# Softmax probabilities and attention heads turned through DRAM in a hybrid decoder layer

## The chip, the cores and the metric

The kernel runs on one core of one Trainium2 chip. The metric is the device time of one execution in microseconds (us); the time before is 1804.2 us, the median of three runs (1803.72 to 1804.21). Besides those runs there is one profiled execution, from which all durations below are read.

Engine names in the rows: PE is TensorE (matrix products and transposes by a product with the identity), DVE is VectorE, ACT is ScalarE, POOL is GpSimd, SP is SyncE, which here only issues DMAs. Each engine works through its own list of instructions strictly in order.

## The reference

One decoder layer on x (256 tokens, width 2048) and a memory of 256 tokens:

```python
x = x + 0.5 * swiglu(rms_norm(x, ffn1_norm), ffn1_gate, ffn1_up, ffn1_down)    # FFN a, inner width 5632

h = rms_norm(x, mix_norm)
fq, fk, fv, f_logit, sq, sk, sv, mq = split(h @ w_in)        # 768,768,768,6,768,256,256,512 columns
fq, fk = rms_norm per head (128 wide)                        # group A: 6 heads
out_a  = causal softmax(fq fk^T * scale + c[t] - c[s]) fv    # c = cumsum(log_sigmoid(f_logit + bias))
sq, sk = rms_norm per head                                   # group B: 6 query heads, 2 key/value heads
out_b  = softmax over a window of 128 (+ ALiBi, + a sink logit in the denominator) sv
mk, mv = rms_norm(mem) @ w_mem_k, rms_norm(mem) @ w_mem_v    # group C: 4 heads into the memory
mq, mk = rms_norm per head
out_c  = softmax(mq mk^T * scale) mv
x = x + concat(out_a, out_b, out_c) @ w_out
x = x + 0.5 * swiglu(rms_norm(x, ffn2_norm), ffn2_gate, ffn2_up, ffn2_down)    # FFN b
```

All in float32. Both attention products need their operands with the contracted index on the partitions: the heads of q and k as (128 of the head, tokens), and the probabilities as (keys, queries). They come out of the products before them the other way round, so they have to be transposed: this is what the change is about.

## The kernel before

**Weights.** Every projection streams its weight from HBM in groups of two 128-row tiles (`load_w`, L212): SP issues one DMA into `raw` (4 buffers, L218), ACT rounds it to `hi` (3 buffers, L220), DVE computes `lo = raw - hi` (3 buffers, L221). TensorE makes float32 accuracy of three faster products: for each of two 128-token tiles and each weight tile x_hi·hi (L315), x_hi·lo (L316) and x_lo·hi (L317), 12 matmuls in a group. So TensorE can't begin a group before ACT has cast it, nor pass the first product before DVE has its `lo`; and ACT can cast a group only once TensorE has left the group three before it, whose `hi` buffer it takes.

**Stages.** FFN a; then the mix stage (about 728 to 985 us): projections mk, mv (of the memory), mq, sqa, skv, sqb, fqa, fka, fqb, fkb, fva, fvb, eight groups each, 512 columns wide for the first three and skv, about 384 for the others; then w_out (wo); then FFN b.

**Attention beside the projections.** Small work is written as generators: `lanes.run` starts a free one, `lanes.put` queues an item for one of two lanes with the names it needs. After each weight group `lanes.tick()` steps every one of them, and a `yield n` skips n ticks. From this program order a scheduler of the framework makes the order on each engine when the kernel is compiled; at run time nothing can be overtaken on an engine.

**Heads.** When a projection is complete in PSUM, `heads_T` (L540) takes for every head and token tile a square with a row sum on ACT (L549, `junkh`; six in a 384-wide projection), a 14-step rsqrt on DVE (L201 to L210 and L554), a scaled copy to `q` on ACT (L559), the transposes on TensorE back into PSUM (L565), and a copy with the gain out of PSUM into `qkv` or `mkT` (L567).

**Probabilities.** A softmax item (`logits`, L676; `mem_stages`, L757) holds one lane from its logits (s_w, s_f, s_m) through maximum (L692), exponentials (L707, L774), normalising (L631), TensorE transposes of the probabilities (L717, L783: pt_w, pt_f, pt_m) and a copy from PSUM. For the sliding window (w0, w2, w4) and the memory (m0, m2) the same item goes on to the values (o_w, o_m) and to `mixT`.

**Turning through DRAM.** The kernel before already uses another transpose for FFN activations and for x: `turn_out` (L256) does 32x32 block transposes on DVE (L262) and writes four DMAs to DRAM (`far`, L268); one DMA reads them back (`turn_in`, L274) so that a strided read (`turned`, L278) gives the transpose. All five DMAs go on SP's queue, the one that also loads all weights.

Of the kernel before, what the change touches and what calls it, by code (L numbers as in the profile page):

```python
# [8 lines left out]
F32 = mybir.dt.float32  # L9
# [69 lines left out]

@with_exitstack  # L80
def hybrid_layer(ctx, tc, x, mem, ffn1_norm, ffn1_gate, ffn1_up, ffn1_down, mix_norm, mem_norm,
# [33 lines left out]
    graw1 = cpool.tile([NK, P], F32, name="graw1")  # L115
# [37 lines left out]
    tri = tri3[:, 0:P]  # L153
# [102 lines left out]
    def turn_out(tmp, src, name):  # L256

        for t in range(NT):  # L260
# [275 lines left out]
    with tc.tile_pool(name="mix", bufs=1, reuse_waits="tile") as mx, \  # L536
# [3 lines left out]
        def heads_T(acc, nh, r, gi, dst, name, off=0):  # L540

            q = mt.tile([P, 4 * SEQ], F32, tag="q", name=f"q_{name}").rearrange("p (t w) -> p t w", t=NT)
            s = small.tile([P, NT, 4], F32, tag="hs", name=f"hs_{name}")
            cols = lambda h: slice(off + h * HD, off + (h + 1) * HD)
            nc.vector.memset(s, 1.0)
# [10 lines left out]
            yield 2  # L556
            for t in range(NT):
# [4 lines left out]
            tv = acc.rearrange("p a b -> p (a b)")[:, :nh * SEQ].rearrange("p (h s) -> p h s", h=nh)  # L562
            for h in range(nh):
                for t in range(NT):
# [8 lines left out]
        def turn_tile(n):  # L573
            return mt.tile([P, 4 * SEQ], F32, tag="q" if n.startswith("out") else "s", name=f"turn_{n}")

        def turns_x1():
            raws = [turn_tile(f"in_x1{c}") for c in range(2)]
            for c in range(2):
                nc.sync.dma_start(*turn_in(raws[c], fars[c]))
            far3 = yield from turn_out(turn_tile("out_x13"), xchunk(3), "x13")  # L580
            for c in range(2):
                yield from scaled(x1T, raws[c], 4 * c, G_MIX)
                raws.append(turn_tile(f"in_x1{c + 2}"))
                nc.sync.dma_start(*turn_in(raws[c + 2], (fars + [far3])[c + 2]))
            for c in (2, 3):
                yield from scaled(x1T, raws[c], 4 * c, G_MIX)
# [38 lines left out]
        def normalise(p, sm, segs, name):  # L625
# [3 lines left out]
            for i in range(2):  # L629
                for t in range(NT):  # L630
                    nc.vector.tensor_scalar(out=p[:, i, segs[t]], in0=p[:, i, segs[t]],  # L631
                                            scalar1=ri[:, t, i:i + 1], scalar2=None, op0=ALU.mult)
# [33 lines left out]
        def logits(tag, h0, qT, kT, fox, name):  # L666
# [8 lines left out]
            else:  # L675
                s = mt.tile([P, 4 * SEQ], F32, tag="s", name=f"ss_{name}")  # L676
                s = s.rearrange("p (i s) -> p i s", i=2)[:, :, 0:3 * P]
# [20 lines left out]
            yield 3  # L698
            if not fox:
                es = small.tile([P, NT, 2], F32, tag="es", name=f"es_{name}")  # L700
                nc.vector.tensor_tensor(out=es, in0=nm,
                                        in1=sink6[:, None, h0:h0 + 2].to_broadcast([P, NT, 2]),
                                        op=ALU.add)
                nc.scalar.activation(es, es, AF.Exp)
            for i in range(2):
                for t in range(NT):
                    nc.scalar.activation(s[:, i, SEG[t]], s[:, i, SEG[t]], AF.Exp,  # L707
                                         bias=nm[:, t, i:i + 1], accum_out=sm[:, t, i:i + 1])
            yield 3
            if not fox:  # L710
                nc.vector.tensor_tensor(out=sm, in0=sm, in1=es, op=ALU.add)
            normalise(s, sm, SEG, name)
            yield 1
# [5 lines left out]
            pTs[name] = s  # L719
            nc.scalar.copy(s, pp[:, :, 0:3 * P])  # L720
            yield 1

        pTs = {}

        def values(tag, h0, v, mix0, name):
# [17 lines left out]
        def swa_pair(h0):  # L743
# [4 lines left out]
            def stages(tag):  # L748
                yield from logits(tag, h0, lambda h: sqT[:, h, :], lambda h: skT[:, h // 3, :], False,
                                  f"w{h0}")  # L750
                yield from values(tag, h0, v, 6, f"w{h0}")
            return stages

        def mem_pair(h0):
            return lambda tag: mem_stages(tag, h0)

        def mem_stages(tag, h0):  # L757
# [6 lines left out]
            nm = small.tile([P, 2, NT], F32, tag="nmm", name=f"nm_{name}")  # L764
            yield 2
            nc.vector.tensor_reduce(out=nm, in_=sp.rearrange("p i (t s) -> p i t s", t=NT), axis=AX.X,
                                    op=ALU.max, negate=True)
            s = mt.tile([P, 4 * SEQ], F32, tag="s", name=f"ss_{name}").rearrange("p (i s) -> p i s", i=2)
            sm = small.tile([P, NT, 2], F32, tag="sm", name=f"sm_{name}")
            segs = [slice(t * SEQ, (t + 1) * SEQ) for t in range(NT)]  # L770
            yield 1
            for i in range(2):
                for t in range(NT):
                    nc.scalar.activation(s[:, i, segs[t]], sp[:, i, segs[t]], AF.Exp,  # L774
                                         bias=nm[:, i, t:t + 1], accum_out=sm[:, t, i:i + 1])
            yield 1
            normalise(s, sm, segs, name)
            yield 3
            pp = psum(tag, f"pt_{name}")
            for i in range(2):  # L780
                for t in range(NT):
# [124 lines left out]
```

## Time and profile before

| what | value |
|---|---|
| median of three runs | 1804.2 us |
| the profiled execution's own time | 1803.99 us |
| its span, first to last instruction | 1802.3 us |
| TensorE busy | 1792.4 us, 99% |
| VectorE busy | 976.4 us, 54% |
| ScalarE busy | 845.7 us, 47% |
| granted TensorE clock, mean | 1.00 |

The profiled execution is 0.2 us from the median; 1.7 us of its time lie outside the span. In a timeline row the first number is the start in us from the span's start, the second the time in us until the end (of all, where a row merges several), and brackets give the idle time of that engine before the row and what ended it. Neighbouring rows overlap, since engines are pipelined: the pitch from start to start is what work costs in a series. The granted clock 1.00 is the upper of TensorE's two levels, 2.4 GHz.

### The profile page before, as it was taken

What the parts mean: (1) busy time and instruction counts of PE and PEld (TensorE: products, weight loads), DVE (VectorE), ACT (ScalarE), POOL (GpSimd) and SP (SyncE); (2) the same over time, 40 slices, a digit from 0 to 9 for tenths busy, and PEclk for the clock granted to TensorE, in tenths of its full rate; (3) what the DMA queues carried; (4) which work ended last, traced back from release to release, by engine and by line L of the source; (5) the groups of instructions that cost most, each with busy time, mean ns of one, the idle gap of its engine ahead of it and who ended that gap; (6) DMA issues with size and microseconds to landing.
All of it is one profiled execution on the core that took longest, in us unless ns stands there. A gap on an engine that the chain in (4) does not pass through costs nothing.

```text
span 1802.3 us, 21677 instructions
## 1 busy us (share of the span) xinstructions
PE 1792.4 (99%) x8170; PEld 1507.2 (84%) x8170; DVE 976.4 (54%) x1197; ACT 845.7 (47%) x1149; POOL 12.1 (1%) x31
## 2 busy tenths in 40 slices
PE   9999999999999999999999999999999999999998
PEld 7888888888888888888999888888888888888887
DVE  5555555555555564645665565555555555544443
ACT  6444444444445443656666454444444444433332
POOL 2000000000000000000000000000000000000000
PEclk9999999999999999999999999999999999999999
DMA  7777777777787777765656586777777777666663
GB/s 240 217 219 214 220 214 218 217 216 218 227 252 234 231 220 239 223 176 152 183 151 185 176 257 188 217 216 222 222 225 223 217 219 214 218 200 198 206 205 128
DMA packets 228025, 379.16 MB, mean 210 GB/s; under 512 B 13834, under 2 KB 65360, under 8 KB 227792
## 3 DMA queue, kind: packets, MB, share of 16 engines
q1 hardware_dynamic: 226512, 375.36, 68.8%
q8 instruction: 64, 1.05, 0.2%
q0 software_dynamic: 528, 1.22, 0.2%
q10 hardware_dynamic: 880, 1.19, 0.2%
q14 instruction: 41, 0.34, 0.1%
HBM read 358.31 MB, written 19.41 MB: 210 GB/s over the span
## 4 chain that ended last, share of the span: by engine, by line
PE 98%; DVE 1%; ACT 1%; DMA 0%; issue 0%; POOL 0%; DVEq 0%; POOLq 0%; ACTq 0%
PE ua L316 4%; PE ua L317 4%; PE gb L317 4%; PE ub L317 4%; PE gb L315 4%; PE ub L315 4%; PE gb L316 4%; PE ub L316 4%; PE ua L315 4%; PE da L316 4%; PE db L316 4%; PE db L315 4%; PE da L317 4%; PE db L317 4%; PE da L315 4%; PE ga L316 4%
## 5 line engine op out<-in xcount | busy, mean ns | idle before, releaser
L221 DVE TENSOR_TENSOR lo_bd<-raw_bd,hi_bd 128x1024 fp32r<-128x1024 f32 x88 | 107.7, 1224 | 122.6 <-ACT hi_bd L220 122.5
L221 DVE TENSOR_TENSOR lo_bu<-raw_bu,hi_bu 128x1024 fp32r<-128x1024 f32 x88 | 107.8, 1225 | 119.5 <-ACT hi_bu L220 119.5
L221 DVE TENSOR_TENSOR lo_au<-raw_au,hi_au 128x1024 fp32r<-128x1024 f32 x88 | 107.8, 1225 | 114.2 <-ACT hi_au L220 114.2
L221 DVE TENSOR_TENSOR lo_ad<-raw_ad,hi_ad 128x1024 fp32r<-128x1024 f32 x88 | 107.5, 1223 | 104.7 <-ACT hi_ad L220 104.6
L220 ACT CAST hi_bd<-raw_bd 128x1024 fp32r<-128x1024 f32 x88 | 92.8, 1055 | 145.5 <-PE db L317 140.5
L221 DVE TENSOR_TENSOR lo_bg<-raw_bg,hi_bg 128x1024 fp32r<-128x1024 f32 x88 | 107.4, 1220 | 96.4 <-ACT hi_bg L220 95.6
L220 ACT CAST hi_bg<-raw_bg 128x1024 fp32r<-128x1024 f32 x88 | 92.8, 1055 | 142.1 <-PE gb L317 86.5
L221 DVE TENSOR_TENSOR lo_ag<-raw_ag,hi_ag 128x1024 fp32r<-128x1024 f32 x86 | 104.9, 1220 | 93.8 <-ACT hi_ag L220 92.9
L220 ACT CAST hi_ad<-raw_ad 128x1024 fp32r<-128x1024 f32 x88 | 92.8, 1054 | 131.7 <-PE da L317 121.5
L220 ACT CAST hi_ag<-raw_ag 128x1024 fp32r<-128x1024 f32 x86 | 90.7, 1055 | 135.9 <-PE ga L317 83.2
L220 ACT CAST hi_bu<-raw_bu 128x1024 fp32r<-128x1024 f32 x88 | 92.8, 1054 | 105.2 <-PE ub L317 78.9
L220 ACT CAST hi_au<-raw_au 128x1024 fp32r<-128x1024 f32 x88 | 92.5, 1054 | 102.6 <-PE ua L317 79.1
L316 PE MATMUL da<-lo_ad,hT_a 128*128 128x512 f32 x352 | 137.0, 389 | 0.8 <-DVE lo_ad L221 0.8
L316 PE MATMUL ua<-lo_au,x0T 128*128 128x512 f32 x352 | 137.0, 389 | 0.3 <-DVE lo_au L221 0.3
L316 PE MATMUL gb<-lo_bg,x2T 128*128 128x512 f32 x352 | 137.0, 389 | 0.0
L315 PE MATMUL gb<-hi_bg,x2T 128*128 128x512 f32 x352 | 136.9, 389 | 0.0
L317 PE MATMUL ua<-hi_au,x0T 128*128 128x512 f32 x352 | 136.9, 389 | 0.0
L315 PE MATMUL da<-hi_ad,hT_a 128*128 128x512 f32 x352 | 136.9, 389 | 0.0
L317 PE MATMUL da<-hi_ad,hT_a 128*128 128x512 f32 x352 | 136.9, 389 | 0.0
L317 PE MATMUL gb<-hi_bg,x2T 128*128 128x512 f32 x352 | 136.9, 389 | 0.0
L315 PE MATMUL ub<-hi_bu,x2T 128*128 128x512 f32 x352 | 136.9, 389 | 0.0
L316 PE MATMUL ub<-lo_bu,x2T 128*128 128x512 f32 x352 | 136.9, 389 | 0.0
(478 smaller groups left out, 3934.9 us busy)
## 6 DMA issues: line engine op xcount, KB each, us to landing
raw_au<-in_ffn_up_dram SPq DMA_DIRECT2D x88, 512.0 KB, 4.5
raw_ad<-in_ffn_down_dram SPq DMA_DIRECT2D x88, 512.0 KB, 5.0
raw_bg<-in_ffn_gate_dram SPq DMA_DIRECT2D x88, 512.0 KB, 4.5
raw_bu<-in_ffn_up_dram SPq DMA_DIRECT2D x88, 512.0 KB, 4.4
raw_bd<-in_ffn_down_dram SPq DMA_DIRECT2D x88, 512.0 KB, 4.6
raw_ag<-in_ffn_gate_dram SPq DMA_DIRECT2D x86, 512.0 KB, 4.5
raw_wo<-in_w_out_dram SPq DMA_DIRECT2D x16, 512.0 KB, 5.2
far_a<-turn_out_a SPq DMA_DIRECT2D x44, 128.0 KB, 2.6
```

The costliest lines, as they stand in the source:

```text
L220: nc.scalar.copy(h, r)
L221: nc.vector.tensor_tensor(out=l, in0=r, in1=h.bitcast(F32), op=ALU.subtract)
L315: nc.tensor.matmul(acc[:, t, :w], hi, wh, start=first, stop=False)
L316: nc.tensor.matmul(acc[:, t, :w], hi, wl, start=False, stop=False)
L317: nc.tensor.matmul(acc[:, t, :w], lo, wh, start=False, stop=last)
```

## The change

The same numbers are computed. Eight of the nine head transposes (all but fkb) and the probabilities of m0, m2, w0, w2, w4 and f0 (not f2, f4) leave TensorE: they are turned by DVE and DMAs through DRAM, as the FFN activations are. Logits and values become separate lane items, so a softmax's lane is free while the turn is under way. A class `Slots` hands out the buffers (one `q`, two `s`, two `turn`) in the order in which they were asked for. The third chunk of x1T is turned in place in a `turn` tile. To make room, `junk`, `junkh` and the first gain load share one buffer, `ones` becomes a slice of `tri3`.

```diff
+class Slots:
+    def __init__(self, n):
+        self.n, self.asked, self.taken, self.back = n, 0, 0, set()
+    def take(self):
+        i, self.asked = self.asked, self.asked + 1
+        while self.taken < i or i >= self.n and i - self.n not in self.back:
+            yield 1
+        self.taken += 1
+        return i
+    def give(self, i):
+        self.back.add(i)
...
-            junk = small.tile([P, 512], F32, tag="junk", bufs=2, name="junk")
+            junk = small.tile([P, 512], F32, tag="junk", bufs=1, name="junk")
...
+        slots = {"q": Slots(1), "s": Slots(2), "turn": Slots(2)}
+        def take(tag, name):
+            i = yield from slots[tag].take()
+            return i, mt.tile([P, 4 * SEQ], F32, tag=tag, bufs=slots[tag].n, name=name)
+        def turn(src, name, out):
+            i, tmp = yield from take("turn", f"turn_{name}")
+            far = yield from turn_out(tmp, src, name, 1)
+            nc.sync.dma_start(*turn_in(tmp, far))
+            yield 3
+            yield from out(tmp)
+            slots["turn"].give(i)
...
-                    junk = small.tile([P, HD], F32, tag="junkh", bufs=2, name="junkh")
+                    junk = small.tile([P, 512], F32, tag="junk", bufs=1, name="junkh")[:, 0:HD]
...
-            tv = acc.rearrange("p a b -> p (a b)")[:, :nh * SEQ].rearrange("p (h s) -> p h s", h=nh)
-            for h in range(nh):
-                for t in range(NT):
-                    nc.tensor.transpose(tv[:, h, t * P:(t + 1) * P], q[:, t, h * HD:(h + 1) * HD], ident)
-            yield 1
-            nc.scalar.activation(dst, tv, AF.Copy, scale=gT[:, G_HEAD + gi:G_HEAD + gi + 1])
+            def out(tmp):
+                nc.scalar.activation(dst.rearrange("p h (c s) -> p h c s", s=32), turned(tmp, NT, nh), AF.Copy,
+                                     scale=gain)
+                yield 1
+            i, tmp = yield from take("turn", f"turn_{name}")
+            stages = turn_out(tmp, q, name, 1)
+            yield next(stages)
+            slots["q"].give(iq)
+            far = yield from stages
+            nc.sync.dma_start(*turn_in(tmp, far))
+            yield 3
+            yield from out(tmp)
+            slots["turn"].give(i)
...
+        def turn_p(s, name):
+            flat = s.rearrange("p i s -> p (i s)")
+            def out(tmp):
+                nc.scalar.copy(flat.rearrange("p (k c s) -> p k c s", c=4, s=32),
+                               turned(tmp, 1, flat.shape[1] // P))
+                yield 1
+            yield from turn(flat[:, None, :], name, out)
...
+            if not by_pe:
+                def rest():
+                    yield from probabilities()
+                    yield from turn_p(s, f"p_{name}")
+                lanes.run(f"p_{name}", rest())
+                return
...
-            lanes.put(f"m{h}", mem_pair(h), ("mk", "mv", "mq"))
+            lanes.put(f"ml{h}", mem_logits(h), ("mk", "mq"))
+            lanes.put(f"m{h}", mem_values(h), (f"p_m{h}", "mv"))
...
-        lanes.put("w0", swa_pair(0), ("sqa", "sk", "sv"))
+        lanes.put("wl0", swa_logits(0), ("sqa", "sk"))
...
+        for h in (0, 2, 4):
+            lanes.put(f"w{h}", swa_values(h), (f"p_w{h}", "sv"))
```

**The place where fqa follows sqb, ScalarE.** `hi_fqa` with its lowest number is the cast of fqa's first group, the next number its second; `junkh` x6 are sqb's six squares, `q_sqb` its scaled copies. Before:

```order
L225 CAST mixT<-o_m_6550 128x2x256
L220 CAST hi_sqb_6620<-raw_sqb_6619 128x2x384
L220 CAST hi_sqb_6648<-raw_sqb_6647 128x2x384
L220 CAST hi_fqa_6681<-raw_fqa_6680 128x2x384
L220 CAST hi_fqa_6708<-raw_fqa_6707 128x2x384
L567 ACTIVATE qkv<-skv,gT 128x512
L549 ACTIVATE junkh,hs_sqb<-sqb,y_x_5451 128x128 x6
L220 CAST hi_fqa_6732<-raw_fqa_6731 128x2x384
L220 CAST hi_fqa_6772<-raw_fqa_6771 128x2x384
```

And of the change, on ScalarE at that place:

```order
L237 CAST hi_sqb_6632<-raw_sqb_6631 128x2x384
L586 ACTIVATE junkh,hs_sqb<-sqb,y_x_5450 128x128 x6
L237 CAST hi_fqa_6657<-raw_fqa_6656 128x2x384
L734 COPY ss_m_6378<-turn_p_m_6602 128x1024
L598 ACTIVATE q_sqb<-sqb,y_sqb 128x128
L237 CAST hi_fqa_6685<-raw_fqa_6684 128x2x384
L598 ACTIVATE q_sqb<-sqb,y_sqb 128x128
L612 ACTIVATE qkv<-turn_sk,gT 128x512
L598 ACTIVATE q_sqb<-sqb,y_sqb 128x128 x2
L237 CAST hi_fqa_6710<-raw_fqa_6709 128x2x384
```

Two casts of fqa stood ahead of sqb's squares, now none does; a turned copy (`ss_m`), two `q_sqb` pieces and a second turned copy stand between the first three casts.

**The same place, VectorE.** `lo_fqa` with its lowest number belongs to fqa's first group; `v_sqb`, `t_sqb`, `y_sqb` are the steps of sqb's rsqrt. Before:

```order
L221 TENSOR_TENSOR lo_sqb_6649<-raw_sqb_6647,hi_sqb_6648 128x2x384
L221 TENSOR_TENSOR lo_fqa_6682<-raw_fqa_6680,hi_fqa_6681 128x2x384
L221 TENSOR_TENSOR lo_fqa_6709<-raw_fqa_6707,hi_fqa_6708 128x2x384
L655 COPY cq<-cps 128x6 x2
L656 TENSOR_SCALAR nck_all<-cps 6x384
L689 SCALAR_TENSOR_TENSOR ss_w_6676<-dist,s_w_6671 128x384 x2
L201 TENSOR_SCALAR v_sqb<-hs_sqb 128x8
L692 TENSOR_REDUCE nm_w_6677<-ss_w_6676 128x2
L202 TENSOR_SCALAR t_sqb<-v_sqb 128x8
```

And of the change, the last steps of the rsqrt on VectorE:

```order
L225 TENSOR_TENSOR t_sqb<-y_sqb 128x8
L226 TENSOR_TENSOR t_sqb<-t_sqb,v_sqb 128x8
L227 SCALAR_TENSOR_TENSOR y_sqb<-t_sqb,y_sqb 128x8
L238 TENSOR_TENSOR lo_fqa_6658<-raw_fqa_6656,hi_fqa_6657 128x2x384
L591 TENSOR_TENSOR y_sqb<-y_sqb,y_x_5450 128x8
L238 TENSOR_TENSOR lo_fqa_6686<-raw_fqa_6684,hi_fqa_6685 128x2x384
L238 TENSOR_TENSOR lo_fqa_6711<-raw_fqa_6709,hi_fqa_6710 128x2x384
```

The first two `lo_fqa` stood ahead of the rsqrt; now the first stands behind its last step but one, and the steps from `v_sqb` on, ahead of the rows shown, follow directly on sqb's last `lo`.

**The same place, SyncE's queue.** `raw_fqa` are the loads of fqa's groups. Before:

```order
L218 DMA raw_sqb_6601<-in_w_in_dram 128x2x384
L218 DMA raw_sqb_6619<-in_w_in_dram 128x2x384
L218 DMA raw_sqb_6647<-in_w_in_dram 128x2x384
L218 DMA raw_fqa_6680<-in_w_in_dram 128x2x384
L218 DMA raw_fqa_6707<-in_w_in_dram 128x2x384
L218 DMA raw_fqa_6731<-in_w_in_dram 128x2x384
```

And of the change, in the same queue:

```order
L235 DMA raw_sqb_6604<-in_w_in_dram 128x2x384
L288 DMA far_p_m_6626<-turn_p_m_6602 32x4x256 x4
L235 DMA raw_sqb_6631<-in_w_in_dram 128x2x384
L288 DMA far_sk<-turn_sk 32x8x64 x4
L235 DMA raw_fqa_6656<-in_w_in_dram 128x2x384
L572 DMA turn_p_m_6602<-far_p_m_6626 128x1024
L235 DMA raw_fqa_6684<-in_w_in_dram 128x2x384
L621 DMA turn_sk<-far_sk 128x2x256
L235 DMA raw_fqa_6709<-in_w_in_dram 128x2x384
```

The first load of fqa stands behind four writes of the memory probabilities and four of the turned keys, which wait for VectorE's transposes.

**From fka's first group to its second, ScalarE.** `hi_fka` are fka's casts, `ss_w` the exponentials of the first sliding-window pair, `ss_m` from `turn_p_m` the copy of the second turned memory probabilities, `mixT` the cast of the memory's values. Before:

```order
L220 CAST hi_fka_6893<-raw_fka_6892 128x2x384
L220 CAST hi_fka_6928<-raw_fka_6927 128x2x384
L567 ACTIVATE qkv<-sqb,gT 128x768
L549 ACTIVATE junkh,hs_fqa<-fqa,y_x_5451 128x128 x6
L220 CAST hi_fka_6960<-raw_fka_6959 128x2x384
L220 CAST hi_fka_7002<-raw_fka_7001 128x2x384
```

And of the change, on ScalarE between the two casts:

```order
L237 CAST hi_fka_6876<-raw_fka_6875 128x2x384
L784 ACTIVATE ss_w_6826,sm_w_6828<-ss_w_6826,nm_w_6827 128x128
L781 ACTIVATE es_w_7016<-es_w_7016 128x4
L784 ACTIVATE ss_w_6826,sm_w_6828<-ss_w_6826,nm_w_6827 128x256
L784 ACTIVATE ss_w_6826,sm_w_6828<-ss_w_6826,nm_w_6827 128x128
L734 COPY ss_m_6406<-turn_p_m_6782 128x1024
L586 ACTIVATE junkh,hs_fqa<-fqa,y_x_5450 128x128
L784 ACTIVATE ss_w_6826,sm_w_6828<-ss_w_6826,nm_w_6827 128x256
L586 ACTIVATE junkh,hs_fqa<-fqa,y_x_5450 128x128 x5
L242 CAST mixT<-o_m_6985 128x2x256
L598 ACTIVATE q_fqa<-fqa,y_fqa 128x128 x6
L237 CAST hi_fka_6907<-raw_fka_6906 128x2x384
```

Before, fka's first two casts stand in a row, and at most six squares and a copy come between two casts. Now ten other rows stand between the first and the second cast, among them six scaled copies `q_fqa` that wait for fqa's rsqrt.

## Rows read from the trace of the kernel before

**Rows 1.** The page, parts 1 and 4: busy time by engine, the chain by engine
```profile
PE 1792.4 (99%) x8170; PEld 1507.2 (84%) x8170; DVE 976.4 (54%) x1197; ACT 845.7 (47%) x1149; POOL 12.1 (1%) x31
...
PE 98%; DVE 1%; ACT 1%; DMA 0%; issue 0%; POOL 0%; DVEq 0%; POOLq 0%; ACTq 0%
```

**Rows 2.** TensorE's waits: line, releaser, total us, times, longest
```profile
PE wo L316 <- DVE lo_wo L221: 0.6, 1, 0.6
PE sqa L316 <- DVE lo_sqa L221: 0.5, 1, 0.5
```

**Rows 3.** The chain in order of time, 835 to 870 us: start, length, what
```profile
839.50 0.66 PE sqa L565 x6
...
848.84 1.73 PE o_m L792 x8
...
862.70 0.44 PE skv L565 x4
...
866.94 1.31 PE s_w L672 x8
```

**Rows 4.** TensorE's timeline, the same product of two successive 384-wide groups
```profile
898.94 0.33 PE L317 MATMUL fka<-hi_fka,x1T 128*128 128x384 f32 x1
...
901.02 0.33 PE L317 MATMUL fka<-hi_fka,x1T 128*128 128x384 f32 x1
```

**Rows 5.** ScalarE's timeline, 862 to 928 us
```profile
862.74 0.83 ACT L220 CAST hi_fqa<-raw_fqa 128x768 fp32r<-128x768 f32 x1 [1.25 <-PE sqb L317]
...
866.98 0.37 ACT L549 ACTIVATE junkh<-sqb,y_x 128x128 f32<-128x128 f32 x1 [2.83 <-PE sqb L317]
...
869.05 0.86 ACT L220 CAST hi_fqa<-raw_fqa 128x768 fp32r<-128x768 f32 x1
...
872.53 0.40 ACT L707 ACTIVATE ss_w<-ss_w,nm_w 128x128 f32<-128x128 f32 x1
...
872.93 0.49 ACT L707 ACTIVATE ss_w<-ss_w,nm_w 128x256 f32<-128x256 f32 x1
...
876.91 1.66 ACT L559 ACTIVATE q_sqb<-sqb,y_sqb 128x128 f32<-128x128 f32 x6 [0.97 <-DVE y_sqb L554]
...
883.60 0.90 ACT L567 ACTIVATE qkv<-sqb,gT 128x768 f32<-128x768 f32 x1
...
897.21 0.59 ACT L225 CAST mixT<-o_w 128x512 fp32r<-128x512 f32 x1 [0.43 <-PE o_w L731]
```

**Rows 6.** The grouped view by line and shape: 32x32 transposes of the FFN's turn
```profile
L262 DVE STREAM_TRANSPOSE turn_out_a<-gsa 128x512 f32<-128x512 f32 x22 | 14.2, 687 | 0.0
```

**Rows 7.** VectorE's timeline, 905 to 920 us
```profile
904.35 0.96 DVE L221 TENSOR_TENSOR lo_fqb<-raw_fqb,hi_fqb 128x768 fp32r<-128x768 f32 x1 [1.13 <-ACT hi_fqb L220]
...
909.77 0.17 DVE L201 TENSOR_SCALAR v_fka<-hs_fka 128x8 f32<-128x8 f32 x1 [1.86 <-ACT junkh L549]
...
910.59 0.17 DVE L209 TENSOR_TENSOR t_fka<-t_fka,v_fka 128x8 f32<-128x8 f32 x1
...
912.52 0.16 DVE L208 TENSOR_TENSOR t_fka<-y_fka 128x8 f32<-128x8 f32 x1
912.72 0.17 DVE L209 TENSOR_TENSOR t_fka<-t_fka,v_fka 128x8 f32<-128x8 f32 x1
```

**Rows 8.** SyncE's timeline, four DMA writes of a turn: start, length of issuing
```profile
734.60 1.86 SPq L268 DMA_DIRECT2D far_x<-turn_out_x  x4
```

**Rows 9.** The tile turn_in_x: from its DMA's issue to landing
```profile
DMA to landing us min/median/max: 4.2/5.1/6.8
```

**Rows 10.** ScalarE's timeline, 1035 to 1050 us
```profile
1042.03 1.71 ACT L286 ACTIVATE x2T<-turn_in_x,gT 128x256 fp32r<-128x256 f32 x4 [1.77 <-DMA turn_in_x<-far_x]
1045.74 1.05 ACT L220 CAST hi_wo<-raw_wo 128x1024 fp32r<-128x1024 f32 x1 [2.00 <-DMA raw_wo<-in_w_out_dram]
```

**Rows 11.** TensorE's timeline, the opening
```profile
6.47 2.04 PE L374 MATMUL ga<-hi_ag,x0T 128*128 128x512 f32 x4 [0.24 <-DVE x0T L246]
...
12.61 0.40 PE L315 MATMUL ga<-hi_ag,x0T 128*128 128x512 f32 x1
```

More of the change, by code (lines that the diff above doesn't have):

```diff
@@ L114, in hybrid_layer @@
     xv = x.rearrange("(t p) d -> p t d", p=P)
-    graw1 = cpool.tile([NK, P], F32, name="graw1")
+    junk1 = small.tile([P, 512], F32, tag="junk", bufs=1, name="graw1")
+    graw1 = junk1[0:NK, 0:P]
     def load_x(queue, k0, nk):
@@ L556, in heads_T @@
             yield 2
+            iq, q = yield from take("q", f"q_{name}")
+            q = q[:, 0:NT * nh * HD].rearrange("p (t w) -> p t w", t=NT)
             for t in range(NT):
@@ L571, in hybrid_layer @@
         x1T = mx.tile([P, NK, 2, SEQ], F32R, name="x1T")
-        def turn_tile(n):
-            return mt.tile([P, 4 * SEQ], F32, tag="q" if n.startswith("out") else "s", name=f"turn_{n}")
         def turns_x1():
-            raws = [turn_tile(f"in_x1{c}") for c in range(2)]
+            raws = []
             for c in range(2):
-                nc.sync.dma_start(*turn_in(raws[c], fars[c]))
-            far3 = yield from turn_out(turn_tile("out_x13"), xchunk(3), "x13")
-            for c in range(2):
[L582 to L586, printed above, removed]
+                raws.append((yield from take("s", f"in_x1{c}")))
+                nc.sync.dma_start(*turn_in(raws[c][1], fars[c]))
+            i3, out3 = yield from take("turn", "out_x13")
+            far3 = yield from turn_out(out3, xchunk(3), "x13")
+            nc.sync.dma_start(*turn_in(out3, far3))
+            for c in range(2):
+                yield from scaled(x1T, raws[c][1], 4 * c, G_MIX)
+                slots["s"].give(raws[c][0])
+                if c == 0:
+                    i2, raw2 = yield from take("s", "in_x12")
+                    nc.sync.dma_start(*turn_in(raw2, fars[2]))
+            yield from scaled(x1T, raw2, 8, G_MIX)
+            slots["s"].give(i2)
+            yield from scaled(x1T, out3, 12, G_MIX)
+            slots["turn"].give(i3)
         lanes.run("x1T", turns_x1())
@@ L675, in logits @@
             else:
-                s = mt.tile([P, 4 * SEQ], F32, tag="s", name=f"ss_{name}")
-                s = s.rearrange("p (i s) -> p i s", i=2)[:, :, 0:3 * P]
+                held[name], s = yield from take("s", f"ss_{name}")
+                s = s[:, 0:6 * P].rearrange("p (i s) -> p i s", i=2)
             nm = small.tile([P, NT, 2], F32, tag="nm", name=f"nm_{name}")
@@ L697, in logits, with probabilities @@
                                         op=ALU.min)
[L698 to L713, printed above, removed]
+            pTs[name] = s
+            def probabilities():
+                yield 3
+                if not fox:
+                    es = small.tile([P, NT, 2], F32, tag="es", name=f"es_{name}")
+                    nc.vector.tensor_tensor(out=es, in0=nm,
+                                            in1=sink6[:, None, h0:h0 + 2].to_broadcast([P, NT, 2]),
+                                            op=ALU.add)
+                    nc.scalar.activation(es, es, AF.Exp)
+                for i in range(2):
+                    for t in range(NT):
+                        nc.scalar.activation(s[:, i, SEG[t]], s[:, i, SEG[t]], AF.Exp,
+                                             bias=nm[:, t, i:i + 1], accum_out=sm[:, t, i:i + 1])
+                yield 3
+                if not fox:
+                    nc.vector.tensor_tensor(out=sm, in0=sm, in1=es, op=ALU.add)
+                normalise(lambda i, t: s[:, i, SEG[t]], sm, name)
+                yield 1
+            if not by_pe:
[3 more added lines that the diff above has]
+                lanes.run(f"p_{name}", rest())
+                return
+            yield from probabilities()
             pp = psum(tag, f"pt_{name}")
@@ L746, in v, with mem_logits @@
                 return sv[:, 0, g * HD:(g + 1) * HD], sv[:, 1, g * HD:(g + 1) * HD]
[L748 to L754, printed above, removed]
+            return lambda tag: values(tag, h0, v, 6, f"w{h0}")
+        def mem_logits(h0):
             return lambda tag: mem_stages(tag, h0)
@@ L764, in mem_stages @@
             nm = small.tile([P, 2, NT], F32, tag="nmm", name=f"nm_{name}")
+            held[name], s = yield from take("s", f"ss_{name}")
+            s = pTs[name] = s.rearrange("p (i s) -> p i s", i=2)
+            part = lambda i, t: s[:, i, :].rearrange("p (k t s) -> p t k s", k=2, t=NT)[:, t]
             yield 2
@@ L817, in hybrid_layer @@
         for h in (2, 4):
-            lanes.put(f"w{h}", swa_pair(h), ("sqa", "sqb", "sk", "sv"))
+            lanes.put(f"wl{h}", swa_logits(h), ("sqa", "sqb", "sk"))
+        for h in (0, 2, 4):
+            lanes.put(f"w{h}", swa_values(h), (f"p_w{h}", "sv"))
         for half, (a, b) in (("a", (0, 3)), ("b", (3, 6))):
@@ L856, in hybrid_layer @@
             if c < 3:
-                lanes.run(f"bT{c}", turn_chunk(x2T, xchunk(c), turn_tile, 4 * c, G_FFN2, f"x2{c}"))
+                lanes.run(f"bT{c}", turn(xchunk(c), f"x2{c}", lambda tmp, c=c: scaled(x2T, tmp, 4 * c, G_FFN2)))
             else:
```

120 lines of the change are left out of this document (67 added, 53 removed).

## Prediction

> **What bounds the kernel now.** I read the page first: TensorE is busy 99% of the span and is 98% of the chain [rows 1]. So a product taken off TensorE shortens the kernel, and a wait put on TensorE lengthens it, each by its own length. The list of TensorE's waits came second: in the mix stage it holds one wait, 0.5 us at sqa for a `lo`, and 0.6 us at wo [rows 2]. The chain in order of time prices what the change removes: six transposes take 0.66 us and four 0.44 us [rows 3], 0.11 us each.
>
> The timelines show what keeps the waits so few. A 384-wide weight group takes TensorE 2.08 us (901.02 minus 898.94) [rows 4]. ScalarE's cast of fqa's first group, at 862.74, waited for TensorE's last use of a buffer and not for its data [rows 5], and sqb's squares came only at 866.98: two casts lay ahead of a block of small work, about two groups of cover for TensorE, before that block began. Reading the change is therefore reading whether its blocks on ScalarE and VectorE are longer than the casts ahead of them.
>
> **Removed.** Fifty transposes of heads (mk 8, mq 8, sqa 6, sk 4, sqb 6, fqa 6, fka 6, fqb 6) and forty of probabilities (w0, w2, w4 18; m0, m2 16; f0 6): 90 x 0.109 = 9.8 us. The wait of 0.5 us at sqa [rows 2] may go too, since the blocks there are cut differently. Together 10.3 us.
>
> The Trainium skill, page "VectorE: DVE Perf Modes", section "The three transpose paths", gives 390 ns for a 128x128 transpose on TensorE (bf16) and advises TensorE for it. By that figure 90 of them would be an estimated 35 us, and with the waits below the kernel would come out near 1795. The rows, where they follow one another, give 0.11, and decide; I give the figure less than 1%, within rival A.
>
> **Added off TensorE.** A 128x512 block transpose on VectorE is 687 ns [rows 6]; 11,520 columns are turned (6,400 of heads, 5,120 of probabilities), 15.5 us on an engine that is busy 54% of the span [rows 1]. ScalarE has as many copies as before, from SBUF instead of PSUM. SyncE gets 14 turns of five DMAs. As totals all this is covered. What isn't covered is order: an engine can't overtake, and a turn makes the loads of weights, the casts and the `lo` wait in line.
>
> **Moved: the casts.** I walk ScalarE and VectorE through the order of the changed kernel with durations of [rows 5, 7]: six squares 2.07 us (869.05 minus 866.98), a cast 0.83, an exponential about 0.5 (872.93 minus 872.53 is 0.40 for 128 columns; 0.49 and its row sum make 0.6 for 256), six scaled copies 1.66, a copy of 768 columns 0.90, the cast into `mixT` 0.59, a `lo` 0.96. The rsqrt's 14 steps: five start within 0.82 (910.59 minus 909.77), the others at 0.20 (912.72 minus 912.52), so 2.6 with its last, 2.4 without. Normalising and adding a mask pass 768 columns in pieces: by the `lo`'s rate 1.0, with the starts of four pieces about 1.4 (an estimate). E is the end of the projection named.
>
> 1. fqa's first group, E of sqb. Squares until E+2.15, cast until E+3.0; VectorE has the rsqrt ahead of the `lo`: E+4.6, and with the `lo` E+5.55. TensorE has only one product to do before it: it waits 5.4. The second cast needs a turned copy and a `q_sqb` that waits for the rsqrt: E+6.9, `lo` E+7.8, against TensorE's end of the first group at E+7.4: about 0.5 more. Sum 6.0, of which 5.4 depends on no landing.
> 2. fka's second group, E of fqa. VectorE starts w0's maximum behind fka's first `lo`, so ScalarE's exponentials fall around E; then the copy of m2, squares to E+4.0, the `mixT` cast E+4.6. VectorE's rsqrt has the `lo` of `mixT` in its midst: it ends at E+7.5. Scaled copies E+9.15, cast E+9.9. TensorE has the first group 2.08, the memory's values 1.73 [rows 3] and half of w2's logits 0.65, E+4.5: 5.4 for the cast and 0.7 for the `lo`, 6.1. Were the exponentials, the copy and the `lo` of `mixT` done early, squares, rsqrt, scaled copies and cast alone would still end at E+7.4: 3.0 + 0.9 = about 4.
> 3. fqb's fourth group, E of fka. Six squares and two exponentials with a cast, E+4.0; normalising and rsqrt E+7.0; scaled copies and the turned copy of fqa between them E+9.7; cast E+10.5. TensorE's cover is three groups, 6.2: it waits 4.3 + 0.9 = 5.2, at least 3.6.
> 4. fkb's fourth group, E of fqb. The turned copy of fka stands behind squares, five exponentials and scaled copies, E+9.8; f0's logits on TensorE need it and are due at E+7.5, after w0's values (1.3, as eight products of w's logits [rows 3]) and three groups: 2.3, and 0.2 for the pipeline's ends. Then VectorE does f0's four additions and its maximum, two such passes of 1.4, ahead of the `lo`: 2.8, as TensorE has only the logits in hand; 0.7 in the next two groups. Sum about 6, at least 3.
> 5. fva's fourth group: squares, `mixT`, scaled copies: 1.4, at least 0. Three smaller places (skv, sqb, fvb), 0.7 each at most: 2.0, at least 0.
>
> The waits: 6.0 + 6.1 + 5.2 + 6.0 + 1.4 + 2.0 = 26.7 us; with every lower bound 5.4 + 4 + 3.6 + 3 = 16. I take the walk, since it uses the order as it stands; its parts are priced from neighbouring rows.
>
> **The sum.** The profiled execution's 1803.99 us (0.2 below the median) - 10.3 + 26.7 = 1820.4 us.
>
> **The queue.** Four writes of a turn take SyncE 1.86 us to issue [rows 8], and the read-back lands 4.2 to 6.8 us after its issue, 5.1 at the median [rows 9]. fqa's first load stands behind the writes of sk's turn, which wait for VectorE; sk's transposes stand behind sqb's seventh `lo`, whose cast takes the buffer of the fourth group, free at E-8.3: cast, `lo`, transposes 0.7 and writes 1.9 lead to an issue near E-3.9 and, with 4.2 to 5.1, to a landing near E+1, ahead of the squares' end. So it adds nothing in the sum. Before has one example of the mechanism: at wo a load behind a turn's DMAs; ScalarE waited 1.77 us for the turned tile and then 2.00 for the weights [rows 10], and it ended as the 0.6 us of TensorE [rows 2]. With one turn and little other work the cover almost held; in the mix stage the turns follow each other.
>
> **Rivals.**
> *A, covered.* The scheduler's blocks meet enough casts ahead, waits stay under the gain, and the kernel is faster: 1803.99 - 10.3 = 1793.7 with none, the border being waits of 10.3 us. For it: before's blocks of squares with a copy between casts cost nothing. Against it: step 1 alone costs 5.4 by dependences, and 16 is the sum of the lower bounds. If step 1 holds and the others shrink to a third of their walk, the sum is 6.0 + 20.7 / 3 = 12.9, still slower. Chance 8% for faster, 4% for within 0.2% (about what a measurement of this kernel can tell from no change).
> *B, late landings.* Read-backs at the far end, 6.8 instead of 5.1 [rows 9], plus as much from four writes: some 2 to 3 us more at steps 2, 3 and 4, where a turned copy stands ahead of a cast. For it: DMAs beside full weight streams; against: in steps 3 and 4 the turned tile was written long before. 1820.4 + 3 x 2.5 = 1828. Chance 14%.
> *C, slow products after a wait.* In the opening four 512-wide products took 2.04 us, 0.46 from start to start, and later ones a pitch of 0.23 [rows 11], the granted clock reading 1.00 throughout; TensorE had done only ten transposes before. If that comes back after each of four waits of 5 us, as much as the opening's slow stretch loses (four products at 0.23 too much, and as many again until the later pitch: 1.8 us) is paid each time: 4 x 1.8 = 7, 1827. Against: all later waits of before are under 1 us, so its rows don't show it. Chance 14%. The Trainium skill, page "TensorE: Matmul & The Clock Gate", section "HAM oscillation — how this bites in real kernels", says that TensorE falls to the lower of its two levels over idle gaps and pays again each time; no run here has such a gap.
>
> **How the numbers follow.** The forecast as it stands, with waits between the lower bounds and the walk plus a few us, has 60%: 1810 to 1824. B and C reach to 1828, both together with their upper sizes to 1833. The lower end takes the lower bounds, 1803.99 - 10.3 + 16 = 1810. The range for 8 in 10 is 1809 to 1831. Faster 0.08, same 0.04, slower 0.88.
>
> **What would show it.** TensorE's waits by line: `lo_fqa`, `hi_fka` or `lo_fka`, `lo_fqb` or `hi_fqb`, the turned fka at f0's logits, `lo_fkb`, each 3 to 6 us; a mix stage about 16 us longer and the FFNs unchanged. TensorE's busy time would be some 10 us less where it isn't stretched by waiting. Wrong would be: the same waits under 10 us in all (A); waits on DMA landings at their head (B); a lower granted clock or doubled pitches behind the waits (C); or a longer FFN, which nothing here explains.

## The result, and the profile after

| | before | after |
|---|---|---|
| median | 1804.2 us (4 runs, 1803.7 to 1804.3) | 1833.4 us (4 runs, 1831.9 to 1836.4) |
| span of the profiled execution | 1802.3 us | 1830.2 us |
| TensorE busy / not busy in the span | 1792.4 / 9.9 us | 1795.0 / 35.2 us |
| mean granted TensorE clock | 1.00 | 0.993 |

The change makes the kernel slower: ratio 1.0164, 95% interval 1.0147 to 1.0182. The page after, parts 1 and 2, answers to [rows 1]:

```profile
PE 1795.0 (98%) x8080; PEld 1505.3 (82%) x8080; DVE 994.0 (54%) x1219; ACT 850.6 (46%) x1149; POOL 11.7 (1%) x31
...
PEclk9999999999999999999899999999999999999999
```

TensorE lost 90 transposes, 9.8 us, and yet is busy 2.6 us longer: its other work takes 12.4 us more. To that come 25.3 us in which it isn't busy. The ledger of the span is -9.8 + 12.4 + 25.3 = 27.9 us. One digit of the granted clock, in the middle, is an 8. TensorE's waits (line, releaser, total us, times, longest) answer to [rows 2]:

```profile
PE fqb L337 <- ACT hi_fqb L237: 4.1, 1, 4.1
PE fqa L337 <- ACT hi_fqa L237: 3.7, 1, 3.7
PE fka L337 <- ACT hi_fka L237: 3.4, 1, 3.4
...
PE sqb L337 <- ACT hi_sqb L237: 2.3, 1, 2.3
PE s_f L746 <- ACT qkv L612: 2.2, 1, 2.2
PE fqa L338 <- DVE lo_fqa L238: 1.9, 1, 1.9
PE s_w L746 <- DVE mixT L243: 1.7, 1, 1.7
PE s_f L746 <- DVE ss_f L758: 1.5, 1, 1.5
...
PE sqb L338 <- DVE lo_sqb L238: 0.7, 1, 0.7
```

These and seven smaller rows of the mix stage sum to 25.1 us, where before had one of 0.5. L337, L338 and L339 are here what L315 to L317 were. The first place, fqa, shows how the waits come about. ScalarE there, to be held against [rows 5]:

```profile
862.68 0.37 ACT L586 ACTIVATE junkh<-sqb,y_x 128x128 f32<-128x128 f32 x1 [5.36 <-PE sqb L339]
...
865.14 0.37 ACT L586 ACTIVATE junkh<-sqb,y_x 128x128 f32<-128x128 f32 x1
...
865.50 0.82 ACT L237 CAST hi_fqa<-raw_fqa 128x768 fp32r<-128x768 f32 x1
...
869.04 0.37 ACT L598 ACTIVATE q_sqb<-sqb,y_sqb 128x128 f32<-128x128 f32 x1 [1.77 <-DVE y_sqb L591]
869.30 0.82 ACT L237 CAST hi_fqa<-raw_fqa 128x768 fp32r<-128x768 f32 x1
```

VectorE at that place:

```profile
865.63 0.17 DVE L218 TENSOR_SCALAR v_sqb<-hs_sqb 128x8 f32<-128x8 f32 x1 [7.32 <-ACT junkh L586]
...
867.86 0.17 DVE L227 SCALAR_TENSOR_TENSOR y_sqb<-t_sqb,y_sqb 128x8 f32<-128x8 f32 x1
867.97 0.96 DVE L238 TENSOR_TENSOR lo_fqa<-raw_fqa,hi_fqa 128x768 fp32r<-128x768 f32 x1
```

And TensorE:

```profile
862.31 0.34 PE L339 MATMUL sqb<-hi_sqb,x1T 128*128 128x384 f32 x1
866.37 0.69 PE L337 MATMUL fqa<-hi_fqa,x1T 128*128 128x384 f32 x1 [3.72 <-ACT hi_fqa L237]
868.98 0.69 PE L338 MATMUL fqa<-lo_fqa,x1T 128*128 128x384 f32 x1 [1.92 <-DVE lo_fqa L238]
869.47 0.52 PE L339 MATMUL fqa<-hi_fqa,x1T 128*128 128x384 f32 x1
869.79 0.52 PE L337 MATMUL fqa<-hi_fqa,x1T 128*128 128x384 f32 x1
...
875.04 0.33 PE L337 MATMUL fqa<-hi_fqa,x1T 128*128 128x384 f32 x1
875.21 0.33 PE L338 MATMUL fqa<-lo_fqa,x1T 128*128 128x384 f32 x1
```

ScalarE waited 5.36 us with nothing to do, until sqb's end released the squares that stood ahead of fqa's first cast; the cast itself then waited for no data. TensorE stood from 862.7 to 866.4, made one product, and stood again until the `lo` behind the rsqrt. No wait of a mix projection's cast in this trace ended at its weight's DMA: the loads had landed, the place in the list was what was late. Afterwards TensorE's products start every 0.32 us until about 873, and every 0.17 later [rows 4]. The granted clock shows why. In the mix stage it is 0.50, which is the lower level, 1.2 GHz, in five stretches, behind the waits at sqb, fqa, fka, fqb and fkb, and 1.00 between them. Their windows (start, end and length; busy us of TensorE, weight loads, VectorE, ScalarE, POOL with the number of instructions; granted clock; DMA share; GB/s):

```profile
849.32:852.74 3.42, 3.42 (x12) 3.42 (x11) 2.22 (x13) 1.77 (x3) 0.00 (x0) 0.50 0.85 226
866.39:873.22 6.83, 4.91 (x14) 4.51 (x15) 4.24 (x13) 4.88 (x11) 0.00 (x0) 0.50 0.78 238
900.52:907.35 6.83, 6.53 (x19) 6.12 (x20) 3.73 (x4) 3.06 (x4) 0.00 (x0) 0.50 0.55 173
931.24:934.66 3.42, 3.06 (x9) 2.66 (x10) 2.69 (x3) 2.07 (x3) 0.00 (x0) 0.50 0.34 95
958.55:961.96 3.41, 3.41 (x11) 3.41 (x12) 2.60 (x6) 2.42 (x6) 0.00 (x0) 0.50 0.64 115
```

TensorE is busy 21.3 us in them. At the upper level the same work would take half of that, so the five stretches cost an estimated 10.7 of the 12.4 us. The pitches of the 384-wide products agree: what they exceed 0.17 by sums to 1.7 us at sqb, 2.0 at fqa, 2.8 at fka, 1.2 at fqb and 1.7 at fkb, 9.4 in all, with other products not counted. The rest of the 12.4 us isn't followed up.

### The profile page after: what moved, and what is told of

It reads as the page before. It is cut to its first block, busy times and chain, and to the rows that moved or that the text cites. A ratio compares the mean times of both kernels' runs of the same rounds, so it can differ in the third digit from the quotient of the medians.

```text
span 1830.2 us, 21603 instructions
## 1 busy us (share of the span) xinstructions
PE 1795.0 (98%) x8080; PEld 1505.3 (82%) x8080; DVE 994.0 (54%) x1219; ACT 850.6 (46%) x1149; POOL 11.7 (1%) x31
## 5 line engine op out<-in xcount | busy, mean ns | idle before, releaser
L338 PE MATMUL da<-lo_ad,hT_a 128*128 128x512 f32 x352 | 137.1, 389 | 0.8 <-DVE lo_ad L238 0.8
L337 PE MATMUL ua<-hi_au,x0T 128*128 128x512 f32 x352 | 137.0, 389 | 0.0
L338 PE MATMUL gb<-lo_bg,x2T 128*128 128x512 f32 x352 | 137.0, 389 | 0.0
L339 PE MATMUL da<-hi_ad,hT_a 128*128 128x512 f32 x352 | 137.0, 389 | 0.0
L339 PE MATMUL ua<-hi_au,x0T 128*128 128x512 f32 x352 | 136.9, 389 | 0.0
L338 PE MATMUL ua<-lo_au,x0T 128*128 128x512 f32 x352 | 136.9, 389 | 0.0
L337 PE MATMUL gb<-hi_bg,x2T 128*128 128x512 f32 x352 | 136.9, 389 | 0.0
L339 PE MATMUL gb<-hi_bg,x2T 128*128 128x512 f32 x352 | 136.9, 389 | 0.0
L337 PE MATMUL da<-hi_ad,hT_a 128*128 128x512 f32 x352 | 136.9, 389 | 0.0
L337 PE MATMUL ub<-hi_bu,x2T 128*128 128x512 f32 x352 | 136.9, 389 | 0.0
```

Of the source, the lines that this page charges most:

```text
L337: nc.tensor.matmul(acc[:, t, :w], hi, wh, start=first, stop=False)
L338: nc.tensor.matmul(acc[:, t, :w], hi, wl, start=False, stop=False)
L339: nc.tensor.matmul(acc[:, t, :w], lo, wh, start=False, stop=last)
```

## The experiments

Times are medians; each was compared with runs of the kernel before on the same chip. L numbers are each kernel's own.

**e1: turns on POOL's queue.**

```diff
-            nc.sync.dma_start(far[:, :, :, a, :]...
+            (queue or nc.sync).dma_start(far[:, :, :, a, :]...
...
-            far = yield from turn_out(tmp, src, name, 1)
-            nc.sync.dma_start(*turn_in(tmp, far))
+            far = yield from turn_out(tmp, src, name, 1, nc.gpsimd)
+            nc.gpsimd.dma_start(*turn_in(tmp, far))
```

> The changed kernel with the five DMAs of each turn of heads, probabilities and x2 in the mix stage issued from POOL's queue instead of SP's; nothing else edited. With that the longest ScalarE work between two casts in the order falls from about 7 us to about 3 us at fka, fqb, fkb. Theory 1 (the turns stand ahead of the weights in SP's queue, so the compiled order puts casts behind blocks of small work, TensorE waits, and its clock falls behind each wait): most of the 25 us of waits and the slow stretches go, 1793 to 1801. Rival (the turns' DMAs slow weight loads and engines by their traffic, whatever queue issues them): about 1830.

Measured 1801.98 us, ratio to before 0.9986 (0.9977 to 0.9996): 31 us under the change with the same DMAs, a little faster than before. The traffic isn't the cause. ScalarE at fqa in this kernel:

```profile
862.72 0.84 ACT L237 CAST hi_fqa<-raw_fqa 128x768 fp32r<-128x768 f32 x1 [1.20 <-PE sqb L339]
864.80 0.37 ACT L586 ACTIVATE junkh<-sqb,y_x 128x128 f32<-128x128 f32 x1 [1.24 <-PE sqb L339]
...
865.16 0.82 ACT L237 CAST hi_fqa<-raw_fqa 128x768 fp32r<-128x768 f32 x1
```

A cast stands ahead of the squares again and others stand between them. It is 1 us above the upper end expected, since sqb's wait stayed. TensorE's longest waits of this kernel in the mix stage:

```profile
PE sqb L337 <- ACT hi_sqb L237: 3.0, 1, 3.0
...
PE sqb L338 <- DVE lo_sqb L238: 0.5, 1, 0.5
PE o_w L813 <- ACT ss_w L734: 0.5, 1, 0.5
```

And VectorE's timeline at sqb:

```profile
840.13 1.96 DVE L698 TENSOR_TENSOR nck_all<-nck_all,cmask 128x384 f32<-128x384 f32 x4 [4.41 <-DMA nck_all<-nck_dram]
...
842.54 0.95 DVE L238 TENSOR_TENSOR lo_sqb<-raw_sqb,hi_sqb 128x768 fp32r<-128x768 f32 x1
843.41 1.22 DVE L854 TENSOR_REDUCE nm_m<-s_m 128x4 f32<-128x1024 f32 x1
```

VectorE waited 4.41 us for the broadcast of the forget gate's sums, to which it adds the mask; sqb's second `lo` and a maximum of the memory's logits (`nm_m`) stood behind. The cast that TensorE waited for is that of sqb's third group (the expectation of e5 calls it the second). On ScalarE it stood behind exponentials of the memory's logits, and the first of them waited 6.26 us for that maximum:

```profile
844.66 0.47 ACT L860 ACTIVATE ss_m<-s_m,nm_m 128x256 f32<-128x256 f32 x1 [6.26 <-DVE nm_m L854]
```

In before the forget gate's sums come later (TensorE starts them at 863.0, in the change at 824.5): the change frees a lane sooner, and the mask's rows move up. No step of my prediction had it.

**e2: the waits filled with products by zero.**

```diff
+                n0, n1 = FILL.get((name, k), (0, 0))
+                fill(acc, aT, n0, done == 0)
                 for j in range(b):
-                    mm_rows(acc, aT, k + j, wh[:, j, :], wl[:, j, :], done == 0, done == nk_all - 1)
+                    mm_rows(acc, aT, k + j, wh[:, j, :], wl[:, j, :], done == 0, done == nk_all - 1,
+                            (lambda: fill(acc, aT, n1, False)) if j == 0 else None)
```

`fill` issues products of a zero matrix with x1T, 256 columns each: n0 of them ahead of a group, n1 behind its first product.

> The changed kernel with products by a zero matrix added on TensorE in five of its waits (sqb second group 18+5, fqa first 31+18, fka second 28+2, fqb fourth 34+3, fkb fourth 12; 256 columns each), sized to fill the waits and not to lengthen them; the order on ScalarE is unchanged. Theory 1 with the clock (TensorE's products after a wait run at the lower level because it had been idle): pitches stay 0.17 behind the filled waits and 8 to 10 us come back, 1822 to 1826. Rival (the slow stretches come from something else, such as contention on buffers by ScalarE and VectorE catching up): pitches of 0.32 remain, 1832 to 1837.

Measured 1824.6 us, 8.8 under the change, as theory 1 has it. TensorE's timeline with the fillers at fqa and the first `lo` product behind them:

```profile
861.91 3.78 PE L349 MATMUL fqa<-x1T,zero 128*64 128x256 f32 x31
...
866.08 2.26 PE L349 MATMUL fqa<-x1T,zero 128*64 128x256 f32 x18
868.18 0.34 PE L340 MATMUL fqa<-lo_fqa,x1T 128*128 128x384 f32 x1
```

The windows of this kernel at that place, columns as above:

```profile
865.00:870.00 5.00, 4.89 (x36) 4.60 (x35) 3.45 (x17) 3.23 (x6) 0.00 (x0) 1.00 0.54 181
870.00:875.00 5.00, 4.84 (x28) 4.52 (x27) 3.75 (x5) 3.76 (x10) 0.00 (x0) 1.00 0.63 150
```

The first `lo` product starts at 868.18, against 868.98 after, most of which sqb's earlier end brings (0.6 us); the granted clock stays at 1.00 here, and products follow at 0.17. The fillers don't cover every wait. At fka 2.5 us are left open, and the clock holds; at fkb a wait of 2.2 us at f0's logits stands ahead of the fillers, and behind it one slow stretch is left, the only one of the mix stage:

```profile
947.42:950.84 3.42, 3.42 (x14) 2.96 (x13) 0.94 (x3) 2.59 (x4) 0.00 (x0) 0.50 0.09 32
```

Half of its 3.42 us taken from the estimate of 10.7 leaves 9.0 us for the other four, and 8.8 were measured. So the slow products come from TensorE's standing still, not from ScalarE and VectorE catching up, and those four stretches cost about 9 us of the 29.

**e3: only the probabilities turned.**

```diff
-                lanes.run(name, heads_T(acc, 3, r1s, g, dst[:, a:b, :], name, by_pe=name == "fkb"))
+                lanes.run(name, heads_T(acc, 3, r1s, g, dst[:, a:b, :], name, by_pe=True))   # default True too
```

> The changed kernel with all nine head transposes on TensorE again and only the probabilities turned (40 transposes less than before, 4.4 us). Theory 1: the long blocks between casts at fqa, fka, fqb, fkb are gone in the order, one of about 9 us is left at skv; 1800 to 1808. Rival (each turn costs the same, so the change's 39 us of loss fall on 14 turns, 2.8 each): 1804 - 4.4 + 6 x 2.8 = 1816.

Measured 1810.3 us (1.0031, 1.0019 to 1.0042): above theory 1, under the rival. Two of TensorE's waits make most of it:

```profile
PE sqb L338 <- DVE lo_sqb L238: 5.7, 1, 5.7
...
PE o_m L877 <- ACT ss_m L734: 1.7, 1, 1.7
```

Nothing is left at fqa, fka, fqb and fkb. The 5.7 us are a `lo` of sqb; which of the mask and the probabilities holds it is what e6 asks.

**e4: only the heads turned.**

```diff
-                                      f"w{h0}", False)
+                                      f"w{h0}", True)      # f0 too
...
-                yield from turn_p(s, f"p_{name}")
+                        nc.tensor.transpose(pp[...], s[...], ident)      # m0, m2: eight each, and the copy
```

> The changed kernel with all probabilities transposed on TensorE again and only the eight head sets turned (50 transposes less than before, 5.5 us). Theory 1: blocks of about 4 us at fqb, fkb and fva and 6 at skv are left between casts; waits of 3 to 10 us, 1802 to 1812. Rival (each turn costs the same): 1804 - 5.5 + 8 x 2.8 = 1821.

Measured 1808.5 us (1.0022, 1.0013 to 1.0031), as theory 1 has it. Its waits in the mix stage are at most 2.1 us. e3 and e4 are 6 and 4 us slower than before, the whole change 29: the cost isn't one per turn. That it grows where heads and probabilities share a list is a reading; no run separates that, and most of e3's loss turns out to be the mask's (e6).

**e5: e1 with the mask pinned behind sqb.**

```diff
-            yield 6
+            yield 10
...
-                nc.vector.tensor_tensor(out=nck_all[:, h, :], in0=nck_all[:, h, :], in1=cmask, op=ALU.add)
+                tc.keep_in_program_order(
+                    nc.vector.tensor_tensor(out=nck_all[:, h, :], in0=nck_all[:, h, :], in1=cmask, op=ALU.add))
```

> The kernel of e1 with the six additions of the causal mask on VectorE pinned to their place in program order and four ticks later, so that they stand behind sqb's lo's instead of ahead of the second one. In e1 VectorE waited 4.4 us there for a broadcast DMA, TensorE 3.0 + 0.5 us at sqb's second group, and its products then ran at half rate (2.2 us). Theory 1: all three go, 5 to 6 us, 1795.5 to 1797.5. Rival (the sqb wait comes from the memory exponentials on ScalarE, and the mask only fills the time): no change, 1801 to 1803.

Measured 1796.1 us, ratio to before 0.9955 (0.9942 to 0.9967): faster than both kernels, by 8.3 and 37 us. TensorE's row of the page:

```profile
PE 1782.9 (99%) x8080; PEld 1496.0 (83%) x8080; DVE 991.5 (55%) x1219; ACT 848.5 (47%) x1149; POOL 62.0 (3%) x116
```

Its longest waits behind the opening:

```profile
PE o_w L814 <- ACT ss_w L735: 1.1, 1, 1.1
PE db L367 <- DVE x_sb L472: 0.8, 1, 0.8
```

TensorE is busy 9.5 us less than before, nearly the 9.8 of the transposes: once nothing is late, the removal is worth what the chain said.

**e6: e3 with the mask pinned** (the edit of e5).

> The kernel of e3 (probabilities alone turned, on SP's queue) with the same pinning of the mask. In e3 TensorE waited 5.7 us for a lo of sqb and 1.7 us for a turned copy, with 2.5 us of slow products. Theory 1: the sqb wait and the slow products go, 1801 to 1803.5, so six turns of probabilities on SP's queue cost little by themselves. Rival (the probabilities' turns delay sqb's lo): 1808 to 1811.

Measured 1801.2 us (0.9983, 0.9973 to 0.9992), in the range of theory 1: the mask held sqb's `lo`, and six turns on SP's queue alone leave some 3 of the 4.4 us, with a wait of 1.7 us for a turned tile at the memory's values still there.

**e7: the change with the mask pinned** (the edit of e5).

> The changed kernel with the same pinning of the mask and nothing else; turns stay on SP's queue. In the changed kernel sqb's waits were 2.3 + 0.7 us and the slow products behind them 1.7 us. Theory 1: about 4.7 us come back there, at most 2 are lost again where the mask now stands between fqa's lo's: 1828 to 1831. Rival (the mask explains most of the loss and the queue little): under 1815.

Measured 1825.4 us, 8 under the change; 3 below the range of theory 1, and far from the rival. The waits moved, too: fqa's two are gone, and two at the memory's values (4.9 us together) came. The mask is the smaller part: e5, which differs from this kernel in the turns' queue alone, is 29 us faster, nearly the 31 between the change and e1. Three casts of this kernel do wait for their loads, 1.5 us at sqb, 1.6 at fkb and 3.6 at fvb, but no wait of TensorE for a weight of these projections is over 0.7 us.

**e8: the casts pinned to program order on ScalarE, the turns on SP's queue.**

```diff
-        nc.scalar.copy(h, r)
+        pin(nc.scalar.copy(h, r))      # tc.keep_in_program_order in mq, sqa, skv, sqb, fqa to fvb
```

> The changed kernel with the casts of the mix projections pinned to program order on ScalarE; turns and weight loads stay together on SP's queue as in the change. In the compiled order the blocks ahead of fka's and fqb's casts shrink from 7.1 and 5.1 us of work to about 2.9 and 2.5; those at fqa, fkb and sqb stay. Theory 1 (the place of the casts in ScalarE's list makes the waits): the waits at fka and fqb with the slow products behind them go, 10 to 14 us, 1819 to 1824. Rival (loads land late behind the turns, wherever the casts stand): ScalarE waits at the casts for DMAs instead, 1830 to 1836.

Measured 1845.8 us, slower by 12; both theories missed. Program order pins a cast behind small work that the free order had let it pass: mq's first cast stands behind the copies of mv and the turned keys now, in ScalarE's timeline:

```profile
775.18 1.26 ACT L678 ACTIVATE mv<-mv,y_mem 128x512 f32<-128x512 f32 x2 [7.06 <-PE mv L342]
777.26 1.15 ACT L615 ACTIVATE mkT<-turn_mk,gT 128x1024 f32<-128x1024 f32 x1 [0.82 <-DMA turn_mk<-far_mk]
778.32 2.92 ACT L240 CAST hi_mq<-raw_mq 128x1024 fp32r<-128x1024 f32 x3
```

TensorE's longest waits there:

```profile
PE mq L340 <- ACT hi_mq L240: 4.3, 1, 4.3
PE fqa L340 <- ACT hi_fqa L240: 3.7, 1, 3.7
```

Again no cast waits for its own DMA, so it speaks against the rival, and at mq it shows the place of the casts at work with the other sign. It doesn't bear out theory 1 where that was to be tested: the wait for fka's cast shrinks (3.4 to 1.5 us), but with the `lo` behind it 3.1 us are left of 3.7 at fka, and 4.2 of 4.4 at fqb. The remedy I had in mind is none.

**e9: two buffers for the squares' unused output** (bfloat16, to fit), on the change. **e10: the same on e5.**

```diff
-            junk = small.tile([P, 512], F32, tag="junk", bufs=1, name="junk")
+            junk = small.tile([P, 512], BF16, tag="junk", bufs=2, name="junk")      # junkh and graw1 too
```

> The changed kernel with two buffers for the squares' unused output instead of one (in bfloat16, so that they fit; the row sums stay float32). In the changed kernel six squares in a row took 2.8 us where before they took 2.07. Theory 1: the squares are back at a pitch of 0.34; five waits get 0.7 us shorter, and the order shrinks the blocks at fqb and fkb a little: 1822 to 1830. Rival (the pitch comes from something else): pitch stays 0.49, 1832 to 1835.

> The kernel of e5 (turns on POOL's queue, mask pinned) with the two bfloat16 buffers of e9. Theory 1: e5 has only 2 us of waits left in the mix stage, so shorter squares have little to give: 1795 to 1797. Rival (squares still bound it): 1793 to 1795.

e9 measured 1832.3 us, the change's own time within its runs and in the rival's range, though the pitch came back as theory 1 has it:

```profile
866.20 0.37 ACT L587 ACTIVATE junkh<-sqb,y_x 128x128 bf16<-128x128 f32 x1 [5.36 <-PE sqb L340]
...
868.28 0.85 ACT L238 CAST hi_fqa<-raw_fqa 128x768 fp32r<-128x768 f32 x1
```

Six squares take 2.08 us instead of 2.82. But the order was compiled anew: fqa's, fka's and fqb's waits are shorter, sqb's grew from 2.3 to 3.4, skv's from 0.6 to 1.2, and the mix stage's sum is 25 us again. e10 measured 1800.3 us (0.9979, against e5's 0.9955, each to before on its own chip), 4 slower than e5 and outside both expectations; its TensorE is busy 2.1 us longer and idle 2.3 longer than e5's, with 1.6 us of it at the memory's values. Why isn't settled.

## Why the prediction came out as it did

The direction was right, and the time, 1833.4, lies 2.4 us above the range.

1. Removed, 9.8 us: right. e5's busy time shows 9.5; I counted 0.5 for sqa's wait besides, and it is gone from the list.
2. The walk of the lists: right in place and nearly in size. Step 1: 3.72 + 1.92 = 5.6 (walked 6.0). Step 2: 1.70 + 3.38 + 0.30 = 5.4 (6.1), of which the walk had put nothing at w2's logits, where the 1.70 stood. Step 3: 4.07 + 0.36 = 4.4 (5.2). Step 4: 2.17 + 1.49 + 0.69 = 4.4 (6). Step 5: 1.25 (1.4). Small places: 4.1 (2.0), since sqb's 3.1 came from the mask. In sum 25.1 against 26.7; no lower bound was undercut. That it is so close is in part luck: the four long steps came 3.5 us under the walk (19.8 against 23.3), and the mask's wait at sqb, where I had 0.7 at most, made up for most of it.
3. The failed step is the sum, which has no term for slow products behind the waits. I had them as rival C, at 14% and 7 us, and took it for an alternative to the forecast. It was a term of the sum: it came with the same waits that I forecast, in five places of which I had walked four in full. The five stretches at the lower clock cost an estimated 10.7 us, and without four of them 8.8 us came back (e2). With the waits as measured and this term the sum is 1820.4 - 1.6 + 10.7 = 1829.5; with all 12.4 us by which TensorE's other work is longer it is 1831.2, against the profiled execution's 1831.9, though this last sum nearly has to close, since the 12.4 are read from that execution's own busy time. What I held against C, that the rows of before show no long wait, was no evidence either way: it only said that the profile couldn't deny it, while the opening's pitch of 0.46 was a row for it [rows 11]. The granted clock of 1.00 that I read there says nothing, since the trace of before has its first record of that clock at 10.1 us; and TensorE had done fifteen transposes by then, not ten.
4. The shared buffer of the squares: I cited 2.07 us for six [rows 5]; with one buffer each waits for the one before, 0.49 apart, 2.82 in all. 0.75 us a place, hidden in the sum by other steps that came out shorter.
5. The queue: as worked out, loads behind the turns landed in time. Rival B, late landings, didn't occur: from mk to fvb no wait of ScalarE in the change ends at a DMA, neither a cast's nor a turned copy's; the first is w_out's first cast (1.1 us). Rival A is out.

What stays open: e1 changes SP's queue and the compiled order together. That the loads weren't late is read from the traces; a kernel with e1's order and turns on SP's queue wasn't tried, and e8, which moved the casts alone, came out slower. Why the compiled order follows the queue isn't shown either.

## What to carry to other kernels

When a busy engine is relieved, read where the compiled lists of the other engines put what it needs next: a turn that costs them nothing in total can still stand ahead of a cast. Price a wait of some us on TensorE with the slow stretch behind it, as a term and not as a case. Try transfers off the critical path in a queue of their own: here POOL's gave 31 us for all turns of heads, probabilities and x2, while the six of the probabilities cost little on SP's once the mask was pinned (e6).

## What the runs showed of the hardware

- Waits from 2.3 + 0.7 us (sqb) to 3.7 + 1.9 (fqa) were each followed by products at 0.32 instead of 0.17 us, 1.2 to 2.8 us lost. Such a wait needn't bring a slow stretch: in e4 2.1 + 0.7 us at sqb were followed by none, and in e7 fkb has the same waits as in the change (2.2 + 1.5 + 0.7) and no stretch behind them. With products by a zero matrix in TensorE's gaps the granted clock stayed at 1.00 at sqb, fqa, fka and fqb (e2).
- Squares with one output buffer run 0.49 us apart, with two 0.35, in e9 as in before, whose output is float32.
- Four writes of a turn take POOL 2.37 us to issue (e1, far_mk at 769.07) against SP's 1.88 for the same tile (after, at 767.07), yet in e1 and e5 TensorE never waits more than 1.1 us for a turned tile.
